# A two-block transformer kernel on one core: operand beginnings, the first weights, a joined recurrence step, and a new order of projections behind the attention

## The chip, the core and the metric

One core of a Trainium2 chip runs the whole program. Its engines are TensorE (PE, with PEld for the loading of weights), VectorE (DVE), ScalarE (ACT), GpSimd (POOL) and SyncE (SP), whose queue issues nearly all DMAs. The metric is the device time of one execution in microseconds (us). Before the change it is 1033.94, the median of three runs (1033.49 to 1034.37).

## What is computed

The input x has 512 positions and 1024 channels, batch 1, fp32. Two blocks follow each other:

```
def first_block(x, ...):
    h = rms_norm(x, g_mix)
    u, gb, gc, q, k, v = split(h @ w_in)
    y_conv = gb * short_conv(gc * u, conv_w)
    y_attn = dilated_mixture(q, k, v)
    x = x + concat(rms_norm(y_conv), rms_norm(y_attn)) @ w_out
    h = rms_norm(x, g_ffn)
    return x + (silu(h @ w_gate) * (h @ w_up)) @ w_down      # 2816 hidden channels

def second_block(x, c, ...):
    shift, scale, gate = split(silu(c) @ w_mod + b_mod)
    h = rms_norm(x) * (1 + scale) + shift
    xa, za, q, k, v, zb, qi, ki, wi, ga, gb = split(h @ w_in)
    ya = gelu(s5_mixer(xa, ...))                             # a complex state-space recurrence
    g = ya @ w_glu + b_glu
    ya = ((g[:, :512] * sigmoid(g[:, 512:])) * silu(za)) @ w_a_o
    yb = (dsa_mixer(q, k, v, qi, ki, wi) * silu(zb)) @ w_b_o # each query keeps its 128 best keys
    x = x + gate * ((sigmoid(ga) * ya + sigmoid(gb) * yb) @ w_out)
    return rms_norm(x, final_g)
```

## The kernel before

**Matrix products.** Nearly all of them run as three products in the type fp32r: a left and a right operand are each split into a high part and the rest, and `mm3` (L187 to L190) adds high x high, high x low and low x high into one PSUM accumulator. One such matmul has a 128x128 weight tile and a moving operand of 512 columns (256 in a few places). The moving operands have names by stage: xh/xl (first norm), fh/fl (feed-forward), th/tl (its hidden channels), hh/hl (second block), sh/sl (state-space output), ybh/ybl, yah/yal, mh/ml (the merged product). Each is a tile of 2048 bytes per partition, and where it begins in a partition follows from the order of the pools and the sizes of what lies in them. Worked out from these sizes, the operands begin at these bytes, modulo 512: the weights and the x, f, h parts at 416, th/tl at 160, sh/sl at 480, mh/ml at 352.

**Weights.** `units()` (L116) is a generator that loads weight blocks of 512 KB in a fixed order through SP (`load_w`, L113), and splits each on ACT (L92) and DVE (L93). `w()` hands out the next one and keeps three ahead; the tiles raw, wh and wl have three buffers each. The very first block is loaded in two halves by `first_w` (L96 to L107): the halves along the columns of the two row tiles that the block has are taken apart, each with its own cast and subtraction.

**Order of the work.** The order on TensorE is the order of the program. On the other engines and on SP a planner orders the instructions ahead of time by when it expects them to be ready, with a raised priority where the program says so. Waits on semaphores then decide when each instruction starts.

**First stage** (`mixer`, L304). Eight blocks x0 to x7 of the input, 256 KB each, come in through two buffers (L328, L329), and ACT and DVE make xh (L338) and xl (L339) of each. The keys' projection, 96 matmuls (L361 to L363), takes the blocks in that order, and with every two of them one weight block. Four small constants (L333 to L336) are issued behind x3.

**Feed-forward** (`ffn`, L554). 22 pairs of projections (j = 0 to 21). Beside them runs `ssm_tables`, a generator of small steps on POOL and DVE that builds the tables of the state-space part; `beside(gen, rate)` (L604) takes so many of its steps per row tile. At j = 0 the squares of the norm are gathered, at j = 2 the norm's factor is spread over the partitions (L226 to L231), and from there `finish` (L583 to L590) reads the accumulators.

**Second block** (`hybrid`, L978). The recurrence (L1121 to L1129) is 63 steps on POOL, each with four operations: a product of 64 columns (hm, L1125), a sum of 32 (hu, L1127), and two sums of 16 each (L1128, L1129) that cross the real and imaginary halves:

```
G.tensor_mul(m, H[:, c - 1, None].to_broadcast([P, 2, 2, 16]), ...)
G.tensor_add(u, m[:, 0], H[:, c])
G.tensor_add(H[:, c, 0], u[:, 0], m[:, 1, 1])
G.tensor_add(H[:, c, 1], u[:, 1], m[:, 1, 0])
```

Meanwhile TensorE runs the attention over four blocks of 128 queries with 8 heads each: scores sc (L249, L250), flips tp (L282), values (L295). Between these it takes steps of a filler, the generator `gates` (L1201 to L1218), at a rate set by `FILLE`; when the attention ends, `drain` takes what is left. `gates` has four projections for szb, four for sza, then the projections t0 to t4 (`tanhs(range(5))`), then four state-space outputs C0 to C3 (`chunk_out`), with t5 behind C0, t6 behind C1, t7 behind C2. One projection is 8 steps of three matmuls, one output chunk is 8 steps of two fp32 matmuls with 64 columns (L1172, L1173). C0 needs the whole recurrence (through the tile hs, L1160).

A chunk first loads two tables of 512 KB, cat (L1166) and tt (L1168), from DRAM through SP; both take the one tag "tab" with two buffers, and so each waits until the matmuls of the chunk before have read theirs. After its matmuls the result goes through ACT and DVE, is stored to DRAM in eight pieces (yad, L1184), read back (yl, L1186) and split into sh and sl (L1188 to L1191).

**Merge and end.** `pair(m)` (L1255) multiplies the attention's output with w_b_o, two columns of blocks at a time, and `glu` (L1263) multiplies sh/sl with w_glu. They run as pair 0, 1, 2, glu, pair 3. Then come the last gates and `pair` with ya, the product with w_out over mh/ml (L1293 to L1330), and the final norm in two halves of 256 positions (`norm`, L1343). Its factor goes through a chain of small DVE operations (L199 to L207), is spread by PE (L231), and multiplies the eight blocks: the first half on POOL with a copy Rs of the factor (L1363), the second on DVE out of PSUM (L1365).

Of the kernel before, what the change touches and what calls it, by code (L numbers as in the profile page):

```python
# [9 lines left out]
F = mybir.dt.float32  # L10
R = mybir.dt.float32r
# [23 lines left out]
class K:  # L35
# [8 lines left out]
    def pool(self, st, name, bufs=1, **kw):  # L44
        if "space" not in kw or kw["space"] == PSUM:
            kw.setdefault("reuse_waits", "tile")
        return st.enter_context(self.tc.tile_pool(name=name, bufs=bufs, **kw))


    def setup(self):  # L50
        nc, a, ctx = self.nc, self.a, self.ctx
        c = self.cpool = self.pool(ctx, "consts")
        self.wpool = self.pool(ctx, "weights")
        self.hpool = self.pool(ctx, "parts")
        self.ps = self.pool(ctx, "psum", space=PSUM)
        self.dram = ctx.enter_context(self.tc.tile_pool(name="scratch", bufs=1, space=DRAM))
        self.ones = c.tile([P, P], F, name="ones")
        self.G.memset(self.ones, 1.0)
        warm = c.tile([P, 1], F, name="warm")
        self.A.activation(warm, self.ones[:, 0:1], AF.Tanh)  # L60
        p = self.tp()
        for _ in range(WARM):
            self.T.matmul(p[:, :P], self.ones, self.ones, start=True, stop=True)
        self.cols = c.tile([P, NCOLS], F, name="cols")
        nc.scalar.dma_start(self.cols, a["cols"])
        self.ident = c.tile([P, P], F, name="ident")
        self.ident_r = c.tile([P, P], R, name="ident_r")
        self.cm = c.tile([P, P], F, name="cm")

    def col(self, name, j):  # L70
        o = COLS[name][0] + j
# [23 lines left out]

    def first_w(self):  # L96

        raw = self.wpool.tile([P, 2, S], F, name="raw", tag="raw", bufs=RAW)
        hi = self.wpool.tile([P, 2, S], R, name="wh", tag="wh", bufs=3)
        lo = self.wpool.tile([P, 2, S], R, name="wl", tag="wl", bufs=3)  # L100
        for k in range(2):
            src = self.a["wqkv"]
            ap = bass.AP(tensor=src.tensor, offset=src.offset + k * S, ap=[[2 * S, P], [1, S]])
            self.nc.sync.dma_start(raw[:, k], ap)
            self.A.copy(hi[:, k], raw[:, k])
            self.V.tensor_sub(lo[:, k], raw[:, k], hi[:, k].bitcast(F))
            yield hi, lo  # L107

    def load_w(self, name, off, kt, n):
        raw = self.wpool.tile([P, kt, n], F, name="raw", tag="raw", bufs=RAW)  # L110
# [5 lines left out]
    def units(self):  # L116

        def cols(name, c0, c1, kt, n):
            for c in range(c0, c1):
                yield self.split_w(self.load_w(name, c * P * kt * n, kt, n))  # L120
        yield from cols("wqkv", 1, 12, 2, S)
        yield from cols("wconv", 0, 12, 8, P)
        yield from cols("wout", 0, 8, 4, 256)
        yield from cols("wgu", 0, 44, 8, P)
        for n in range(8):
            for k0, kt in ((0, 8), (8, 8), (16, 6)):
                yield self.split_w(self.load_w("wdown", (n * 22 + k0) * P * P, kt, P))
        yield from cols("win2", 0, 5, 8, P)
        yield self.split_w(self.load_w("win2v", 0, 8, 72))
        yield from cols("win2", 5, 29, 8, P)  # L130
        yield from cols("wab", 4, 7, 4, 256)
        yield from cols("wglu", 0, 4, 4, 256)
        yield from cols("wab", 7, 8, 4, 256)
        for c in range(4):
            yield from cols("win2", 29 + 2 * c, 31 + 2 * c, 8, P)
            yield from cols("wab", c, c + 1, 4, 256)
        yield from cols("wout2", 0, 8, 8, P)
# [166 lines left out]
    def mixer(self):  # L304
# [16 lines left out]
        sq = sm.tile([P, S], F, name="sqA", tag="sq")  # L321
        first = self.first_w()
        for k in range(8):
            if k < 2:
                unit = next(first)
                if k:
                    self.ahead.append(unit)
            x = t1.tile([P, S], F, name="x", tag="x", bufs=2)  # L328
            nc.sync.dma_start(x, a["xT"][:, k * S:(k + 1) * S])  # L329
            if k in (2, 4):  # L330
                self.ahead.append(next(self.stream))
            if k == 4:
                nc.sync.dma_start(self.ident, a["ident"])  # L333
                nc.sync.dma_start(self.cm, a["cm"])
                nc.sync.dma_start(self.lc, a["lc"])
                nc.sync.dma_start(self.gqk, a["gqk"])  # L336
            g = self.col("g_mix", k)
            A.activation(xh[k], x, AF.Copy, scale=g)  # L338
            V.scalar_tensor_tensor(xl[k], x, g, xh[k].bitcast(F), op0=OP.mult, op1=OP.subtract)  # L339
            if k == 0:  # L340
                A.activation(sq, x, AF.Square)
            else:
                s2 = t1.tile([P, S], F, name="s2", bufs=2)
                A.activation(s2, x, AF.Square)
                G.tensor_add(sq, sq, s2)
        self.A.copy(self.ident_r, self.ident)
        self.mod_start()
        gqk = sm.tile([P, 64], F, name="gqk1")
        V.scalar_tensor_tensor(gqk, self.gqk[:, 0], 0.125, self.gqk[:, 1], op0=OP.mult, op1=OP.mult)
        rx = sm.tile([P, 4], F, name="rx")  # L350
# [203 lines left out]
    def ffn(self, x1):  # L554
# [49 lines left out]
        def beside(gen, rate):  # L604

            for _ in range(8):
                next(gen)
                pace[0] += rate
                if pace[0] >= 1:
                    pace[0] -= 1  # L610
                    next(table, None)
            return self.run(gen)
# [3 lines left out]
        for j in range(22):  # L616
            if j == 0:
                ws, first = [self.w() for _ in range(3)], [self.acc() for _ in range(3)]
                for js, ks in (((0, 1), range(4)), ((2,), range(4)), ((0, 1, 2), range(4, 8))):
                    for k in ks:  # L620
                        for q in js:
                            self.gemm(first[q], ws[q], xs, [k])
                with self.tc.high_priority(offset=LEAD):
                    r = self.rms(wk, [sq], D, "rf")
                continue
            if j == 1:
                first.append(beside(self.proj(xs), 0.25))
                continue
            if j == 2:
                pg = beside(self.proj(xs, self.acc2), 0.25)  # L630
                with self.tc.high_priority(offset=LEAD):
                    Rf = self.spread(wk, r, wk.tile([P, S], F, name="Rf"))
                pu = beside(self.proj(xs, self.acc2), 0.25)
                finish(0, *first[:2])
                finish(1, *first[2:])
                finish(2, pg, pu)
                continue
            ps = []
            for _ in range(2):
                t = self.proj(xs)  # L640
                ps.append(beside(t, 0.25 if j < 4 else 0.36))
            finish(j, *ps)
            if j > NT1:
                self.advance_mod()
# [333 lines left out]
    def hybrid(self, xs, second, close, out):  # L978
# [35 lines left out]
        ap = self.pool(aa, "attnE")  # L1014
        ss = ExitStack()
        ssp = self.pool(ss, "ssm", side="right")
        U = ssp.tile([P, 32, 64], F, name="U")
        H = ssp.tile([P, 64, 2, 16], F, name="H")
        s1 = ExitStack()
# [89 lines left out]
        def chunk_in():  # L1109
# [12 lines left out]
            for c in range(1, 64):  # L1122
                m = ssi.tile([P, 2, 2, 16], F, name="hm", bufs=2)
                u = ssi.tile([P, 2, 16], F, name="hu", bufs=2)
                G.tensor_mul(m, H[:, c - 1, None].to_broadcast([P, 2, 2, 16]),  # L1125
                             self.a8.rearrange("p (w r) g -> p w r g", w=2))
                G.tensor_add(u, m[:, 0], H[:, c])  # L1127
                G.tensor_add(H[:, c, 0], u[:, 0], m[:, 1, 1])  # L1128
                G.tensor_add(H[:, c, 1], u[:, 1], m[:, 1, 0])  # L1129


        def silu2(out, p):
# [68 lines left out]
        def gates():  # L1201
# [6 lines left out]
                for j in js:  # L1208
                    A.activation(thb[j], (yield from self.proj(xs)), AF.Tanh, scale=0.5)

            yield from tanhs(range(5))
            for _ in cin:
                pass
            s1.close()
            sso = self.pool(ss, "ssmout", side="right")
            for c in range(4):
                yield from chunk_out(sso, c)
                yield from tanhs(range(5 + c, min(6 + c, 8)))  # L1218

        sels = [sel, select(2), select(3)]  # L1220

# [60 lines left out]

        ya = []
        for m in range(4):
            if m == 3:
                glu()
            pair(yb, thb[2 * m:2 * m + 2], m, lambda n: thb[n])
        ss.close()
        m1 = thb

# [52 lines left out]
        def norm(e):  # L1343
# [15 lines left out]
                Rs = x3p.tile([P, S // 2], F, name="Rs")  # L1359
                A.copy(Rs, Rl)  # L1360
            for k in range(8):
                if e == 0:
                    G.tensor_mul(x3[k][:, t], x3[k][:, t], Rs)  # L1363
                else:
                    V.tensor_mul(x3[k][:, t], x3[k][:, t], Rl)  # L1365
                if k % 2:
                    nc.sync.dma_start(out.rearrange("(k p) t -> p k t", p=P)[:, k - 1:k + 1, t],
                                      x3t[:, k - 1:k + 1, t])

        for n in range(5, 8):  # L1370
            self.run(last(n, 0))
        self.run(last(5, 1))
        first, second = norm(0), norm(1)
        next(first)
        next(first)
# [108 lines left out]
```

## Time and profile before

| | before |
|---|---|
| median of three runs | 1033.94 us (1033.49 to 1034.37) |
| the profiled execution's own time | 1035.94 us |
| its span, first to last instruction | 1034.2 us |
| mean granted TensorE clock | 0.984 of 2.4 GHz |
| instructions | 13,924 |

The span is what the trace shows; 1.74 us of the profiled execution lie around it. The profiled execution is 2.0 us above the median of the runs. The busy time of a matmul in the trace reaches over the beginning of the next one, so the pace is read from starts, or from a stretch divided by the matmuls in it. A granted clock of 1.00 is 2.4 GHz, 0.50 is 1.2 GHz.

### The profile page before, as it was taken

How to read it: one execution, taken by the hardware profiler on the slowest of the kernel's cores; microseconds unless marked ns; L12 is line 12 of the kernel's file. 1: busy time of each engine (PE TensorE's matmuls, PEld its weight loads, DVE VectorE, ACT ScalarE, POOL GpSimd, SP SyncE). 2: the span in 40 equal slices, each digit the busy share in tenths (PEclk: the TensorE clock that was granted, in tenths of full speed). 3: DMA queues.
4: the chain of work that ended last, by engine and by line, in shares of the span. 5: the costliest groups of instructions: out<-in, count | busy, mean ns of one | idle time of the engine just before them, and what ended most of it. 6: DMA issues, size and time to landing. Idle time of an engine off the chain costs nothing.

```text
span 1034.2 us, 13924 instructions
## 1 busy us (share of the span) xinstructions
PE 998.9 (97%) x5074; PEld 824.7 (80%) x5074; DVE 687.2 (66%) x1315; ACT 424.7 (41%) x717; POOL 170.3 (16%) x393
## 2 busy tenths in 40 slices
PE   8999999999899999999999999999999699999995
PEld 6787777888787778888888898888887588788884
DVE  4876677886898757787743257799984355644434
ACT  6445556534234443233232235544444464433251
POOL 3020121005800000000010000001888200000022
PEclk9999999999999999999999999999999699999998
DMA  7233121124236547455543343373222154433212
GB/s 263 82 120 126 62 82 62 41 82 128 78 125 188 160 141 252 161 200 182 184 152 114 106 132 105 102 120 108 99 82 102 62 152 112 149 118 102 82 42 82
DMA packets 55572, 125.12 MB, mean 121 GB/s; under 512 B 17424, under 2 KB 24080, under 8 KB 55376
## 3 DMA queue, kind: packets, MB, share of 16 engines
q1 hardware_dynamic: 55360, 124.19, 37.7%
q8 instruction: 40, 0.66, 0.3%
q14 instruction: 28, 0.23, 0.1%
q10 hardware_dynamic: 144, 0.05, 0.0%
HBM read 110.45 MB, written 12.58 MB: 119 GB/s over the span
## 4 chain that ended last, share of the span: by engine, by line
PE 71%; POOL 10%; DVE 10%; DMA 3%; issue 3%; ACT 3%; SPq 1%; DVEq 0%; POOLq 0%; ACTq 0%
PE acc L188 19%; PE acc L189 19%; PE acc L190 19%; POOL hm L1125 3%; DVE wl L93 2%; POOL H L1128 2%; POOL hu L1127 2%; PE acc L363 2%; PE acc L361 2%; PE acc L362 1%; DMA x<-in_xT 1%; POOL H L1129 1%; PE acc L295 1%; PE tp L282 1%; POOL stt L719 1%
## 5 line engine op out<-in xcount | busy, mean ns | idle before, releaser
L92 ACT CAST wh<-raw 128x1024 fp32r<-128x1024 f32 x157 | 162.5, 1036 | 286.2 <-PE acc L189 238.4
L93 DVE TENSOR_TENSOR wl<-raw,wh 128x1024 fp32r<-128x1024 f32 x157 | 194.2, 1238 | 89.2 <-ACT wh L92 87.7
L188 PE MATMUL acc<-fh,wh 128*128 128x512 f32 x336 | 133.1, 396 | 1.4 <-DVE gs L585 1.4
L189 PE MATMUL acc<-fl,wh 128*128 128x512 f32 x336 | 130.9, 390 | 0.0
L190 PE MATMUL acc<-fh,wl 128*128 128x512 f32 x336 | 130.8, 389 | 0.0
L188 PE MATMUL acc<-hh,wh 128*128 128x512 f32 (+1 forms) x280 | 114.3, 408 | 0.0
L190 PE MATMUL acc<-hh,wl 128*128 128x512 f32 (+1 forms) x280 | 110.1, 393 | 0.0
L189 PE MATMUL acc<-hl,wh 128*128 128x512 f32 (+1 forms) x280 | 109.9, 392 | 0.0
L188 PEld LDWEIGHTS acc<-fh,wh 128*128 128x128 f32 x336 | 63.1, 188 | 16.3 <-issue 1.9
L190 PEld LDWEIGHTS acc<-fh,wl 128*128 128x128 f32 x336 | 63.1, 188 | 13.5
L189 PEld LDWEIGHTS acc<-fl,wh 128*128 128x128 f32 x336 | 63.1, 188 | 12.7 <-issue 0.2
L188 PE MATMUL acc<-th,wh 128*128 128x512 f32 (+1 forms) x198 | 72.6, 367 | 0.0
L189 PE MATMUL acc<-tl,wh 128*128 128x512 f32 (+1 forms) x198 | 72.3, 365 | 0.0
L190 PE MATMUL acc<-th,wl 128*128 128x512 f32 (+1 forms) x198 | 72.3, 365 | 0.0
L190 PEld LDWEIGHTS acc<-hh,wl 128*128 128x128 f32 (+1 forms) x280 | 52.5, 187 | 12.3
L257 ACT ACTIVATE e<-z,mn 128x128 f32<-128x128 f32 (+3 forms) x64 | 36.0, 562 | 63.9 <-DVE mn L253 63.4
L188 PEld LDWEIGHTS acc<-hh,wh 128*128 128x128 f32 (+1 forms) x280 | 52.7, 188 | 10.7 <-issue 1.4
L189 PEld LDWEIGHTS acc<-hl,wh 128*128 128x128 f32 (+1 forms) x280 | 52.8, 189 | 8.7
L1125 POOL TENSOR_TENSOR hm<-H,a 128x64 f32<-128x64 f32 x63 | 25.8, 410 | 125.7 <-DVE H L243 120.9
L666 POOL TENSOR_TENSOR sqD<-sqD,s 128x512 f32<-128x512 f32 x6 | 8.4, 1394 | 208.6 <-ACT s L653 208.6
L189 PEld LDWEIGHTS acc<-tl,wh 128*128 128x128 f32 x198 | 37.3, 189 | 6.1
L188 PEld LDWEIGHTS acc<-th,wh 128*128 128x128 f32 x198 | 37.3, 189 | 6.0
(402 smaller groups left out, 2153.6 us busy)
## 6 DMA issues: line engine op xcount, KB each, us to landing
raw<-in_wgu SPq DMA_DIRECT2D x44, 512.0 KB, 3.6
raw<-in_win SPq DMA_DIRECT2D x37, 512.0 KB, 3.6
mraw<-in_wmod SPq DMA_DIRECT2D x24, 512.0 KB, 4.6
raw<-in_wout SPq DMA_DIRECT2D x16, 512.0 KB, 3.5
raw<-in_wdown SPq DMA_DIRECT2D x16, 512.0 KB, 3.4
raw<-in_wconv SPq DMA_DIRECT2D x12, 512.0 KB, 3.5
raw<-in_wqkv SPq DMA_DIRECT2D x11, 512.0 KB, 4.1
x<-in_xT SPq DMA_DIRECT2D x16, 256.0 KB, 5.2
```

The lines of the kernel that those rows point to most:

```text
L92: self.A.copy(hi, raw)
L93: self.V.tensor_sub(lo, raw, hi.bitcast(F))
L188: self.T.matmul(out, lh, rh, start=start, stop=False)
L189: self.T.matmul(out, lh, rl, start=False, stop=False)
L190: self.T.matmul(out, ll, rh, start=False, stop=stop)
L257: self.A.activation(e[:, :n], z[:, :n], AF.Exp, bias=mn, scale=-1.0, accum_out=den)
L282: self.T.transpose(pp[:, j * P:(j + 1) * P], e[:, j * P:(j + 1) * P], self.ident)
L361: T.matmul(ps[i], xh[k][:, t], wh[:, kk], start=k == 0, stop=False)
L363: T.matmul(ps[i], xl[k][:, t], wh[:, kk], start=False, stop=k == 7)
L1125: G.tensor_mul(m, H[:, c - 1, None].to_broadcast([P, 2, 2, 16]), self.a8.rearrange("p (w r) g -> p w r g", w=2))
L1127: G.tensor_add(u, m[:, 0], H[:, c])
L1128: G.tensor_add(H[:, c, 0], u[:, 0], m[:, 1, 1])
```

## The change

- A helper `pad` puts a dummy tile on POOL into four pools (constants 96 bytes, smallA 448, ssm 480, x3E 352), so that the pools and tiles behind it begin at multiples of 512 bytes.
- `first_w` loads the first two weight blocks in four pieces of 256 KB, one per row tile and half; the input blocks get three buffers; the third weight block is issued at k = 4, and the four small constants at k = 7. The order of the wab and wglu blocks follows the new order of the merge.
- The feed-forward's projection j = 1 runs without table steps, and j = 3 takes 0.5 steps per row tile where it took 0.25.
- The two 16-column sums of the recurrence become one of 32 columns with a reversed operand.
- `gates` takes t0 to t6 ahead of C0; t7 follows C0, and C1, C2, C3 follow without a projection between them.
- The four attention pairs run ahead of `glu`.
- The final norm's first half is multiplied on DVE (with Rs) instead of POOL.

```diff
+    def pad(self, pool, size):
+        self.G.memset(pool.tile([P, size // 4], F, name="pad"), 0.0)
...
     def first_w(self):
-        raw = self.wpool.tile([P, 2, S], F, name="raw", tag="raw", bufs=RAW)
-        hi = self.wpool.tile([P, 2, S], R, name="wh", tag="wh", bufs=3)
-        lo = self.wpool.tile([P, 2, S], R, name="wl", tag="wl", bufs=3)
-        for k in range(2):
-            src = self.a["wqkv"]
-            ap = bass.AP(tensor=src.tensor, offset=src.offset + k * S, ap=[[2 * S, P], [1, S]])
-            self.nc.sync.dma_start(raw[:, k], ap)
-            self.A.copy(hi[:, k], raw[:, k])
-            self.V.tensor_sub(lo[:, k], raw[:, k], hi[:, k].bitcast(F))
-            yield hi, lo
+        src = self.a["wqkv"]
+        for c in range(2):
+            raw = self.wpool.tile([P, 2, S], F, name="raw", tag="raw", bufs=RAW)
+            hi = self.wpool.tile([P, 2, S], R, name="wh", tag="wh", bufs=3)
+            lo = self.wpool.tile([P, 2, S], R, name="wl", tag="wl", bufs=3)
+            for k in range(2):
+                ap = bass.AP(tensor=src.tensor, offset=src.offset + (c * P * 2 + k) * S, ap=[[2 * S, P], [1, S]])
+                self.nc.sync.dma_start(raw[:, k], ap)
+                self.A.copy(hi[:, k], raw[:, k])
+                self.V.tensor_sub(lo[:, k], raw[:, k], hi[:, k].bitcast(F))
+                yield hi, lo
...
-        yield from cols("wab", 4, 7, 4, 256)
+        yield from cols("wab", 4, 8, 4, 256)
         yield from cols("wglu", 0, 4, 4, 256)
-        yield from cols("wab", 7, 8, 4, 256)
...
-            if k < 2:
+            if k < 4:
                 unit = next(first)
-                if k:
+                if k % 2:
                     self.ahead.append(unit)
-            x = t1.tile([P, S], F, name="x", tag="x", bufs=2)
+            x = t1.tile([P, S], F, name="x", tag="x", bufs=3)
...
-            if k in (2, 4):
+            if k == 4:
                 self.ahead.append(next(self.stream))
-            if k == 4:
+            if k == 7:
                 nc.sync.dma_start(self.ident, a["ident"])
...
             if j == 1:
-                first.append(beside(self.proj(xs), 0.25))
+                first.append(self.run(self.proj(xs)))
...
-                ps.append(beside(t, 0.25 if j < 4 else 0.36))
+                ps.append(beside(t, 0.5 if j < 4 else 0.36))
...
-                G.tensor_add(H[:, c, 0], u[:, 0], m[:, 1, 1])
-                G.tensor_add(H[:, c, 1], u[:, 1], m[:, 1, 0])
+                G.tensor_add(H[:, c], u, m[:, 1, ::-1])
...
-            yield from tanhs(range(5))
+            yield from tanhs(range(7))
...
                 yield from chunk_out(sso, c)
-                yield from tanhs(range(5 + c, min(6 + c, 8)))
+                yield from tanhs(range(7 + c, 8))
...
         for m in range(4):
-            if m == 3:
-                glu()
             pair(yb, thb[2 * m:2 * m + 2], m, lambda n: thb[n])
+        glu()
...
             for k in range(8):
-                if e == 0:
-                    G.tensor_mul(x3[k][:, t], x3[k][:, t], Rs)
-                else:
-                    V.tensor_mul(x3[k][:, t], x3[k][:, t], Rl)
+                V.tensor_mul(x3[k][:, t], x3[k][:, t], Rl if e else Rs)
```

## Rows read from the trace of the kernel before

**Rows 1.** The page's first part: busy time and share of the span of each engine.

```profile
PE 998.9 (97%) x5074; PEld 824.7 (80%) x5074; DVE 687.2 (66%) x1315; ACT 424.7 (41%) x717; POOL 170.3 (16%) x393
```

**Rows 2.** Waits of TensorE: line waiting, what ended it, us in total, times, longest.

```profile
PE acc L1172 <- POOL hs L1160: 10.3, 1, 10.3
PE tp L231 <- DVE rey L205: 5.4, 2, 5.0
...
PE acc L361 <- ACT xh L338: 2.2, 3, 1.1
PE tp L282 <- ACT qT L241: 1.9, 1, 1.9
PE acc L188 <- DVE gs L585: 1.4, 1, 1.4
PE tp L231 <- DVE sc_p L777: 1.3, 1, 1.3
...
PE acc L189 <- DVE sl L1191: 0.6, 1, 0.6
```

**Rows 3.** Windows: length, PE, PEld, DVE, ACT, POOL busy (count), PE clock, DMA share, GB/s.

```profile
5.33:31.13 25.80, 24.15 (x97) 17.42 (x97) 14.63 (x18) 16.65 (x26) 9.93 (x7) 1.00 0.72 247
116.80:124.00 7.20, 5.28 (x19) 4.01 (x18) 5.84 (x13) 4.16 (x9) 2.19 (x1) 0.76 0.22 73
282.87:304.63 21.76, 21.76 (x97) 18.02 (x96) 21.76 (x30) 8.14 (x12) 0.92 (x2) 1.00 0.35 121
802.90:823.40 20.50, 13.43 (x53) 12.26 (x54) 7.42 (x20) 8.87 (x18) 5.88 (x25) 0.50 0.21 74
809.95:819.59 9.64, 9.62 (x42) 9.24 (x43) 3.85 (x10) 3.70 (x9) 0.00 (x0) 0.50 0.15 56
830.33:835.52 5.19, 5.19 (x45) 5.02 (x44) 3.46 (x10) 4.26 (x9) 0.00 (x0) 1.00 0.49 145
857.44:860.93 3.49, 3.49 (x34) 3.49 (x32) 3.48 (x8) 3.24 (x6) 0.00 (x0) 1.00 0.50 65
982.88:999.68 16.80, 16.80 (x74) 13.54 (x73) 6.67 (x7) 8.63 (x16) 4.66 (x3) 1.00 0.21 63
```

**Rows 4.** Timeline of SP in the first stage: start, length, the third input block's issue.

```profile
6.14 0.33 SPq L329 DMA_DIRECT2D x<-in_xT  x1
```

**Rows 5.** POOL by line: the first of the recurrence's two sums.

```profile
L1128 POOL TENSOR_TENSOR H<-hu,hm 128x16 f32<-128x16 f32 x63 | 18.1, 287 | 4.9
```

**Rows 6.** Timeline of SP behind chunk C1, and the landing of all tt tables.

```profile
835.88 0.43 SPq L1168 DMA_DIRECT2D tt<-tabs  x1
842.11 3.83 SPq L1184 DMA_DIRECT2D yad<-ys  x8
847.63 0.34 SPq L1186 DMA_DIRECT2D yl<-yad  x1
...
DMA to landing us min/median/max: 4.5/5.0/5.7
```

**Rows 7.** Timeline of DVE in the feed-forward: a table step with its wait.

```profile
268.98 0.26 DVE L840 TENSOR_SCALAR snr<-pr 128x48 f32<-128x48 f32 x1 [4.41 <-POOL pr L811]
```

**Rows 8.** Timeline of the final norm: one DVE step of each half, then both multiplications.

```profile
1014.03 0.17 DVE L200 TENSOR_SCALAR rey<-rev 128x2 int32<-128x2 int32 x1
...
1023.41 0.65 DVE L200 TENSOR_SCALAR rey<-rev 128x2 int32<-128x2 int32 x1
...
1019.89 5.49 POOL L1363 TENSOR_TENSOR x<-x,Rs 128x256 f32<-128x256 f32 x8 [16.79 <-ACT Rs L1360]
...
1028.10 2.74 DVE L1365 TENSOR_TENSOR x<-x,tp 128x256 f32<-128x256 f32 x8 [1.38 <-PE tp L231]
```

**Rows 9.** Groups of PE matmuls by form, of L188 alone (L189, L190 alike).

```profile
L188 PE MATMUL acc<-fh,wh 128*128 128x512 f32 x336 | 133.1, 396 | 1.4 <-DVE gs L585 1.4
...
L188 PE MATMUL acc<-hh,wh 128*128 128x512 f32 x272 | 111.1, 409 | 0.0
...
L188 PE MATMUL acc<-mh,wh 128*128 128x512 f32 x40 | 15.8, 395 | 0.0
```

More of the change, by code (lines that the diff above doesn't have):

```diff
@@ L68, in setup @@
         self.cm = c.tile([P, P], F, name="cm")
+        self.pad(c, 96)
     def col(self, name, j):
@@ L120, in cols @@
                 yield self.split_w(self.load_w(name, c * P * kt * n, kt, n))
-        yield from cols("wqkv", 1, 12, 2, S)
+        yield from cols("wqkv", 2, 12, 2, S)
         yield from cols("wconv", 0, 12, 8, P)
@@ L347, in mixer @@
         self.mod_start()
+        self.pad(sm, 448)
         gqk = sm.tile([P, 64], F, name="gqk1")
@@ L1016, in hybrid @@
         ssp = self.pool(ss, "ssm", side="right")
+        self.pad(ssp, 480)
         U = ssp.tile([P, 32, 64], F, name="U")
@@ L1372, in hybrid @@
         self.run(last(5, 1))
+        self.pad(x3p, 352)
         first, second = norm(0), norm(1)
```

## The prediction

> **What bounds the kernel now.** I read the busy time first: TensorE is busy for 97% of the span, every other engine far less [rows 1], so a change pays only where TensorE stands still, where its clock is down, or where a matmul takes longer than it must. The table of TensorE's waits says where it stands still: one wait of 10.3 us of the first chunk matmul (L1172) for hs, 5.0 us at the end for the norm's factor, 2.2 us in three waits for the input, and 1.3 and 1.4 us at the start of the feed-forward [rows 2]. The windows say where the clock is down: behind the 10.3 us wait the granted clock is 0.50, the lower level of 1.2 GHz, for 20.5 us [rows 3], and C0's piece takes 9.64 us where C1's, which holds as many matmuls of the same kinds, takes 5.19 at 1.00 [rows 3]. A much shorter wait, 1.9 us of L282 [rows 2], is also followed by a fall: 0.76 over the 7.20 us around it [rows 3]. So a wait of TensorE has two prices, its own length and the slow work behind it. The pace comes last: 96 matmuls of 512 columns in 21.76 us are 226.7 ns each in a steady stretch, and 72 in 16.80 us over mh/ml 233.3 [rows 3] (a record or two over that number overlap the edges).
>
> **Part by part, against the profiled execution's own 1035.94 us.**
>
> *A, the start.* The keys' 96 matmuls take 25.80 us, where 96 x 0.2267 = 21.76 would do [rows 3]: 4.0 us are lost, 2.2 of them in three waits for xh [rows 2]. The third block's load is issued only at 6.14 us [rows 4], because it needs a buffer that x0 holds. With three buffers it goes out right behind the sixth piece, and the pieces by row tile put 256 KB less in front of it; the constants, now behind the last block, are out of the way too. Against that, SP issues two DMAs more, and ACT and DVE each make two smaller pieces of what was one. Bounds: 0 and -4.0. I take **-2.0**, nearly the row of waits.
>
> *B, table steps in the feed-forward.* The waits of 1.3 and 1.4 us [rows 2] come while DVE sits in front of table steps that wait for POOL, one of them 4.41 us with `finish` queued behind it [rows 7]. Without steps beside j = 1 these are later; but the planner may put them in front of the norm or of `finish` all the same, and the doubled rate at j = 3 brings them closer together. Bounds: both waits gone, -2.7, or one more like the longer, +1.4. I take **-0.6**, the middle.
>
> *C, the order behind the attention.* Counting the filler's steps, TensorE now runs t5 and t6, with attention between, ahead of C0: together some 16 us, as t5 and t6 hold 48 matmuls of 512 columns, 48 x 0.2267 = 10.9 us, and the attention the rest. hs was 10.3 us late, so that wait goes, whatever the joined sum costs: it replaces two, of which the first takes 18.1 us over 63 steps [rows 5] and the second about as much, and even were it as long as both, 16 us cover it. This part is **-10.3**. With it goes the slow clock: 9.64 - 5.19 = 4.45 us at C0, and in t5 the 3.8 us from 819.6 to 823.4 that ran at half, so 1.9 us: **-6.35**.
>
> What is late next? C2 and C3 now follow directly on C1 and C2, and cat and tt share two buffers. C1's piece ends at 835.52 [rows 3]; at once SP issues cat, at 835.88 tt, and tt lands 5.0 us later (4.5 to 5.7) [rows 6]. So far t6 and t7 covered that; now nothing stands between, so TensorE waits some 5.2 us twice: **+10.4** (0.36 + 4.5 to 0.36 + 5.7 each: 9.7 to 12.2). The splitting into sh/sl and the copies into hs fit beside it. Each wait also has the second price. The 1.9 us wait cost 7.20 x 0.24 = 1.7 us of clock, the 10.3 us one 6.35 [rows 3]; at 5.2 us a straight line between these gives 3.5, an estimate, twice **+7.0**, which C2, C3 (3.49 us of matmuls [rows 3]) and the first pair would pay. Bounds: 3.4 and 12.7. A fourth pair, 24 matmuls or 5.4 us, now stands between C3 and `glu`, so the wait for sl goes: **-0.6** [rows 2]. C's sum: -10.3 - 6.35 + 10.4 + 7.0 - 0.6 = **+0.15**, bounds -4 and +8.
>
> *D, the end.* In the second half's norm the first four DVE steps take some 0.65 us where the same take 0.17 in the first half, while POOL multiplies (5.49 us) [rows 8]: 4 x 0.48 = 1.9 us on the path of the 5.0 us wait [rows 2]. On DVE the eight products take 2.74 / 8 = 0.34 us each [rows 8]. Some fit ahead of the second half's chain; of the others one or two may stand in it. **-1.2**, bounds -1.9 and -0.5. The four stores of that half leave earlier and hold nobody.
>
> *E, beginnings.* If mh/ml step at 226.7 in place of 233.3 ns, the 3 x 40 full matmuls [rows 9] give 120 x 6.6 = **-0.8**; bounds 0 and -1.0 with a little for sh/sl. Below that see the third rival: no operand in this trace begins at a multiple of 64 bytes, so the pace at 0 is not shown. The four memsets lie on POOL, which is idle for 84% of the span [rows 1]; alone they cost nothing.
>
> *The rest* is the recurrence itself, 9 us earlier on POOL, hidden behind t5 and t6; if these did not cover it, hs would be the wait again.
>
> Sum: -2.0 - 0.6 + 0.15 - 1.2 - 0.8 = **-4.45**, so 1031.5 for the profiled execution. That one stands 2.0 above the median of the runs, so the forecast is **1029.5**. A measurement of this kernel can tell some 0.2%, 2.07 us, from no change: the bounds are 1031.9 and 1036.0.
>
> **The rivals.**
>
> *The clock holds, or the tables are hidden.* If no slow work follows the two table waits, C is -6.85 and the time 1029.5 - 7.0 = 1022.5. Against it: the waits of 1.9 and of 10.3 us were each followed by a fall [rows 2, 3]. If the tables also came in time, it would be 1012.1; but the two buffers exclude a load before the chunk's last matmul, and tt was issued 0.36 us behind it [rows 3, 6].
>
> *SP's queue (slower).* SP issues in a fixed order. If the planner expects C1's result stores before C2's end of reading, cat and tt of the next chunk stand behind the eight yad stores and yl, which were issued 6.6 to 12.1 us behind a chunk's end [rows 6]. Then tt lands at 12.1 + 0.7 + 5.0 = 17.8 us instead of 5.4: +12.4 once, and 1029.5 + 12.4 = 1041.9, slower. It decides from a delay of 6.5 us on, as then the sum passes +2.07. For it: between the chunks lies now less time than the stores take to be ready, so at C3 they are close. Against it: the trace has tt 6.2 us ahead of yad [rows 6].
>
> *The pace (faster).* The pace depends on where a moving operand begins: 226.7 ns at 416 and 233.3 at 352 modulo 512 [rows 3], with the weights at the same place. All of them lie at 32 modulo 64, and the change brings nearly all to 0. If that takes away what is above the 512 columns at 2.4 GHz, 213.3 ns, each matmul gains up to 13.4 ns; fh and hh alone are 3 x (336 + 272) = 1824 [rows 9], so up to -24 us from them and 1005 us; with the other groups lower still. For it: the difference of 6.6 ns exists. Against it: 416 and 160 differ in their place and step alike at 226.7, so the excess may be the weights' or a fixed one. The Trainium skill, "TensorE: Matmul & The Clock Gate", section "Back-to-back issue gap", gives N/2.4 + 2.5 ns, which is 215.8 for 512 columns, and with no condition on where an operand begins; the measured 226.7 stands above it. By that page the sum would be 1824 x 10.9 = -20 us lower from these two groups, 1010. The same section's sustained 131 ns for 512 columns is contradicted by every row here.
>
> *The change does less than it says.* If the planner puts the table steps and the products where they were, B and D are 0, and the forecast becomes 1031.3; this lies within the likeliest case.
>
> **How the numbers follow.** The likeliest, table waits in the stall's place with a slow clock behind them: 0.52, its own range 1024 to 1038 (C from -4 to +8 with the other terms at their values, 1025 to 1037, and a little for these). By its centre I put 0.30 of it below 1031.9, 0.14 between the bounds and 0.08 above. Clock holds or tables hidden: 0.15. Pace: 0.14. SP's queue: 0.15, of which 0.03 is a short delay that ends between the bounds; 0.04 stay for what I don't see, half and half between no difference and slower. Faster 0.59, same 0.19, slower 0.22. The range of 1012 to 1040 leaves out the full pace gain (most of 0.14) and the longer half of the queue's delays (about 0.06).
>
> **What would show it.** Of A: L361's waits gone and the keys' stretch near 23.8 us. Of C: no wait for hs at C0, but two of about 5 us at L1172 or L1173 in front of C2 and C3, ended by tabs, and a granted clock of 0.50 behind them; with the first rival the clock stays at 1.00, with SP's queue cat is issued behind yl. Of D: L199 to L202 at 0.17 us in both halves. Of B: less than 2.7 us in the two feed-forward waits. Of E: mh's stretch of 72 matmuls at 16.3 us; for the pace rival fh's stretch of 96 below 21 us, and that alone would make the forecast wrong by ten and more us.

## The result, and the profile after

The changed kernel takes 1052.84 us (median of four runs, 1050.60 to 1053.51), beside 1033.92 before (four runs here): a ratio of 1.018, 95% interval 1.0164 to 1.0196. It is slower by 18.9 us, where 4.4 us less were forecast, and outside the range. The profiled execution took 1052.63 us, its span is 1050.8. The two profiled executions lie 16.7 us apart, less than the medians, as the one before stands 2.0 above its median.

TensorE's waits after (line waiting, what ended it, us in total, times, longest), to be read beside [rows 2]. Lines are the changed kernel's: L287 is L282 before (a flip, that is a transposition of e on PE), L236 is L231, L903 is L897, L1178 is L1172.

```profile
PE tp L287 <- DVE e L265: 8.2, 2, 8.0
PE acc L1178 <- DMA cat<-tabs: 5.9, 1, 5.9
PE tp L903 <- ACT bts L904: 4.2, 1, 4.2
PE tp L236 <- DVE rey L210: 3.6, 2, 3.2
PE acc L1178 <- ACT ybh L1259: 3.4, 1, 3.4
...
PE tp L1356 <- ACT s L1345: 2.1, 1, 2.1
...
PE acc L193 <- DVE gs L591: 1.5, 1, 1.5
PE tp L236 <- DVE sc_p L783: 1.3, 1, 1.3
```

The wait for hs is gone, and one nearly as long, 8.0 us, stands at a flip of the attention, which waits for e. Two waits for the tables are new (the 3.4 us at L1178 is also C3's, though it is put down to ybh: cat was issued at 866.58 and PE went on at 870.17; in experiment 1 both are put down to cat, 9.3 us). One of 4.2 us in the feed-forward is new too.

Windows after (columns as in [rows 3]):

```profile
5.31:29.05 23.74, 22.87 (x96) 17.82 (x97) 20.41 (x18) 16.42 (x26) 11.32 (x7) 1.00 0.77 266
329.30:336.10 6.80, 5.12 (x19) 3.53 (x20) 3.30 (x4) 3.45 (x8) 0.36 (x1) 0.50 0.32 128
428.49:450.25 21.76, 21.76 (x98) 18.02 (x96) 17.88 (x26) 6.80 (x10) 0.00 (x0) 1.00 0.54 193
800.30:810.50 10.20, 5.78 (x16) 4.86 (x17) 4.88 (x14) 5.89 (x13) 2.42 (x9) 0.50 0.09 34
851.50:865.20 13.70, 9.02 (x54) 8.74 (x56) 2.94 (x7) 4.02 (x6) 0.00 (x0) 0.50 0.37 112
868.60:882.30 13.70, 11.67 (x43) 10.55 (x44) 5.01 (x9) 5.38 (x9) 0.09 (x1) 0.50 0.27 91
992.63:1008.95 16.32, 16.32 (x74) 13.52 (x73) 6.44 (x7) 7.55 (x13) 2.94 (x2) 1.00 0.29 94
```

Each of the four long waits has a stretch at 0.50 with it. In the three of the second block PE is busy for 5.78 + 9.02 + 11.67 = 26.5 us, which at the full clock would be about 12.4 less (a step of 512 columns takes 427 ns there, by the starts from 878.71 to 881.27, beside 226.7). Before it was 13.43 us in one stretch, 6.3 lost.

Where the time went is read from the same matmul in both traces, start against start. At the end of the keys the changed kernel is 2.1 us ahead, at 300 us 2.2 ahead, at 400 us 4.2 behind, at 790 us 4.3 behind, at the beginning of the last gates (906 before, 923 after) 17.5 behind, at the last product's 256-column halves 16.7 to 17.2, at the end of the span 16.6. So two places cost: +6.5 between 300 and 400, +13.2 between 790 and 906.

The wait for the flip, which ends inside the window from 800.30, looks like this (POOL, ACT, DVE and PE of the timeline; start, length, line; in brackets the idle time before and what ended it):

```profile
801.67 0.25 POOL L1135 TENSOR_TENSOR H<-hu,hm 128x32 f32<-128x32 f32 x1
...
801.95 1.24 ACT L246 COPY hs<-H 64x252 f32<-64x252 f32 x2 [13.61 <-POOL H L1135]
803.22 0.61 ACT L262 ACTIVATE e<-z,mn 128x384 f32<-128x384 f32 x1
...
801.95 0.82 DVE L248 COPY hs<-H 64x252 f32<-64x252 f32 x2 [11.50 <-POOL H L1135]
803.96 0.16 DVE L264 RECIPROCAL rd<-den 128x1 f32<-128x1 f32 x1 [1.19 <-ACT e L262]
804.15 0.42 DVE L265 TENSOR_SCALAR e<-e,rd 128x384 f32<-128x384 f32 x1
...
804.72 0.88 PE L287 MATMUL tp<-ident,e 128*128 128x128 f32 x3 [7.97 <-DVE e L265]
```

DVE stands for 11.5 us, not for lack of work, but because the next instruction of its queue is a copy into hs, which needs the recurrence up to its last step but one. ACT stands for 13.6 us in the same way. The softmax's e goes through both engines, its exponent on ACT (L262) and then its division on DVE (L264, L265), and each part is behind that engine's copies. This is not new. Before the change DVE's lines were these:

```profile
808.30 0.84 DVE L243 COPY hs<-H 64x252 f32<-64x252 f32 x2 [13.07 <-POOL H L1129]
809.17 0.17 DVE L259 RECIPROCAL rd<-den 128x1 f32<-128x1 f32 x1
809.37 0.42 DVE L260 TENSOR_SCALAR e<-e,rd 128x384 f32<-128x384 f32 x1
```

PE's wait was put down to hs then, since C0 came first on PE; the flip that follows C0's first step was held by the same copy: e was done at 809.79, and C0 began at 809.97. With other work in C0's place PE would have stood at the flip nearly as long.

### The profile page after: what moved, and what is told of

The parts are those of the page before. It is cut to its first block, busy times and chain, and to the rows that moved or that the text cites. A ratio compares the mean times of both kernels' runs of the same rounds, so it can differ in the third digit from the quotient of the medians.

```text
span 1050.8 us, 13873 instructions
## 1 busy us (share of the span) xinstructions
PE 1005.9 (96%) x5074; PEld 833.2 (79%) x5074; DVE 693.6 (66%) x1324; ACT 423.8 (40%) x718; POOL 155.8 (15%) x326
## 4 chain that ended last, share of the span: by engine, by line
PE 74%; DVE 10%; POOL 9%; issue 3%; DMA 2%; ACT 1%; SPq 0%; DVEq 0%; POOLq 0%; ACTq 0%
PE acc L193 19%; PE acc L194 19%; PE acc L195 19%; POOL hm L1132 2%; DVE wl L98 2%; POOL hu L1134 2%; POOL H L1135 2%; PE acc L369 2%; PE acc L367 2%; PE acc L368 2%; PE acc L300 2%; PE tp L287 1%; DMA tt<-tabs 1%; PE acc L1179 1%; PE acc L1178 1%
## 5 line engine op out<-in xcount | busy, mean ns | idle before, releaser
L193 PEld LDWEIGHTS acc<-fh,wh 128*128 128x128 f32 x336 | 63.5, 189 | 16.6 <-issue 2.1
L262 ACT ACTIVATE e<-z,mn 128x128 f32<-128x128 f32 (+3 forms) x64 | 36.0, 562 | 58.7 <-DVE mn L258 58.3
L195 PEld LDWEIGHTS acc<-th,wl 128*128 128x128 f32 x198 | 37.3, 188 | 6.0
```

Source lines behind the costliest of these rows:

```text
L193: self.T.matmul(out, lh, rh, start=start, stop=False)
L195: self.T.matmul(out, ll, rh, start=False, stop=stop)
L262: self.A.activation(e[:, :n], z[:, :n], AF.Exp, bias=mn, scale=-1.0, accum_out=den)
```

## The experiments

All are edits of the changed kernel if nothing else is said. Medians stand beside that of the kernel before on the same chip, which was 1034.4 to 1036.4; the ratios are to it. "Less" and "more" without another name are against the changed kernel's 1052.84, which was not run again beside them. Runs of one kernel spread by up to 6.6 us (before: 1033.08 to 1039.66), so a difference of 2 us says little, and the single runs of experiments 2 and 4 count by their traces.

**1. The old table rates.**

```diff
-                first.append(self.run(self.proj(xs)))
+                first.append(beside(self.proj(xs), 0.25))
...
-                ps.append(beside(t, 0.5 if j < 4 else 0.36))
+                ps.append(beside(t, 0.25 if j < 4 else 0.36))
```

> The changed kernel with the feed-forward's table rates of before (0.25 at j = 1 and j = 3), nothing else undone. Theory (the faster rate brings the second table's transposes ahead of the landing of the first table's tt store, and PE then waits for the copy bts behind it): the wait of 4.2 us at L903 goes, and with it the half clock of 6.8 us behind it, so about 6.5 us less than the changed kernel, near 1046. Rival (the loss in the feed-forward comes from the pads or from the shifted start, not from the rate): the wait stays and the time is that of the changed kernel, 1052.8.

1045.6 us (1041.6 to 1047.5), 7.2 less; no wait at L903 above 1 us, and no half clock there. The theory holds as to the place.

**2. Two buffers for bts and tt**, at the new rates. These are two tiles of the table building; they share the tag io, which has one buffer.

```diff
-            bts = p.tile([P, 8, P], F, name="bts", tag="io")
+            bts = p.tile([P, 8, P], F, name="bts", tag="io", bufs=2)
...
-            tt = p.tile([P, 8, P], F, name="tt", tag="io")
+            tt = p.tile([P, 8, P], F, name="tt", tag="io", bufs=2)
```

> The changed kernel with two buffers for the tiles bts and tt of the table building (tag io), rates as changed. Theory (bts of the second table has to wait for the store of the first table's tt, which shares its one buffer): the wait of 4.2 us at L903 goes at the new rates too, about 6.5 us less than the changed kernel. Rival (the wait is for DMA in general, the weights loaded in the same microseconds): the wait stays at 3 us or more.

1045.9 us in one run, 6.9 less, and L903 is gone from the waits; behind the tables it is 2.4 us ahead of before, start against start, where the changed kernel is 4.2 behind. So the cause is the one buffer: the second table's copy bts waits for the first table's tt to be stored. In the changed kernel that store was issued by SP at 322.30, with three weight blocks around it, and ACT stood until 330.34:

```profile
330.34 0.58 ACT L904 COPY bts<-tp 128x512 f32<-128x512 f32 x1 [7.11 <-DMA raw<-in_wgu]
```

The releaser named is a weight load. The view of the store's own line (L925) names the copy as what waited for it, and a longest landing of 7.8 us, which from 322.30 ends at 330.1:

```profile
  ACT bts L904: 5.0, 2
...
DMA to landing us min/median/max: 4.3/6.1/7.8
```

Before, the same copy waited for the store too, but only for 0.34 us:

```profile
331.44 0.59 ACT L898 COPY bts<-tp 128x512 f32<-128x512 f32 x1 [0.34 <-DMA tabs<-tt]
```

It was done at 332.03, half a us ahead of PE's next transposes for it (L897, 332.52). At the new rate these were due at 326.75.

**3. The first chunk's copies into hs on POOL.**

```diff
-                    self.copy(hs[64 * ri:64 * ri + 64, e:8:2, 1:],
+                    (G.tensor_copy if c == 0 else self.copy)(
+                        hs[64 * ri:64 * ri + 64, e:8:2, 1:],
```

> The changed kernel with the four copies into hs of the first chunk on POOL instead of ACT and DVE. Theory (the planner put these copies ahead of the attention's work in the fixed queues of ACT and DVE, and both engines stand there until the recurrence ends, so PE waits for e): the 8.0 us wait of PE for e at L265 goes and the half clock behind it too, about 2.9 us of work; 9 to 11 us less than the changed kernel, near 1042 to 1044. Rival (the recurrence itself holds the attention, or the wait for e has another cause): the wait stays, or comes back at C0 as a wait for hs of the same length.

1040.64 us (1038.7 to 1044.1), 12.2 less, a little more than expected. The wait for e is gone (0.3 us) and none for hs has come, though the four copies take 3.64 us on POOL. The blocked queues are shown.

**4. Two sums again in the recurrence.**

```diff
-                G.tensor_add(H[:, c], u, m[:, 1, ::-1])
+                G.tensor_add(H[:, c, 0], u[:, 0], m[:, 1, 1])
+                G.tensor_add(H[:, c, 1], u[:, 1], m[:, 1, 0])
```

> The changed kernel with the recurrence's last step as two sums of 16 columns again, as before the change. Theory of the blocked queues: the recurrence ends some 8 to 9 us later, and the wait for e grows from 8.0 to about 16 to 17 us, with the half clock behind it not shorter: 9 to 12 us more than the changed kernel. Rival (the copies are placed by when the planner expects the recurrence to end, so with four operations it puts them later): the wait for e goes or shrinks, and the time falls by up to 10 us.

1048.52 us in one run, 4.3 less, against my theory and with the rival: the wait for e is 4.9 us instead of 8.0, although the recurrence ends later. In the trace DVE's copy into hs starts at 809.32. Counted in the timelines, 22 of the second block's 32 divisions of e on DVE and 23 of its 32 exponents on ACT stand ahead of the copies here, exactly as in the kernel before; in the changed kernel it is 19 and 19. So the joined sum put the copies three and four steps of the attention further ahead. This fits a planner that places the copies by when it expects the recurrence to end; no run sets its order by hand, so the planner's reason stays an inference. (Start against start, 2.5 us of the gain lie between 790 and 906 and 1.6 between 300 and 400, where the feed-forward's wait is 3.4 instead of 4.2.)

**5. The joined sum alone**, on the kernel before.

```diff
-                G.tensor_add(H[:, c, 0], u[:, 0], m[:, 1, 1])
-                G.tensor_add(H[:, c, 1], u[:, 1], m[:, 1, 0])
+                G.tensor_add(H[:, c], u, m[:, 1, ::-1])
```

> The kernel before with the joined sum alone, nothing else changed. Theory of the blocked queues: the recurrence ends 9 us earlier, the planner puts the copies into hs a little earlier in the queues of ACT and DVE, and as C0 follows at once on PE, the wait falls from 10.3 to 2 to 4 us whichever instruction of PE carries it; with less half clock behind it 8 to 12 us less than before, 1022 to 1026. Rival (the copies move ahead by more than the recurrence gains): the wait is 7 us or more, at L265 instead of L1172, and the time is within 4 us of before.

1030.07 us (1028.7 to 1033.8), ratio 0.9946. The rival was right on the mechanism, and the time lies between: the wait is 7.6 us, and it is at L282 for e, no longer at L1172 for hs. ACT's copies start at 797.05, 11 us earlier than before, with 19 exponents and 19 divisions ahead of the copies in place of 23 and 22, and the wait falls by 2.7 us alone.

**6. The joined sum and the copies on POOL**, on the kernel before.

The edit is that of experiment 5 with that of experiment 3.

> The kernel before with two edits, the joined sum and the first chunk's copies into hs on POOL. Theory of the blocked queues: ACT and DVE go on with the attention while the recurrence ends, so the wait for e of 7.6 us that the joined sum alone showed goes; C0 then waits for hs itself, as the recurrence ends near 798.3 and the four copies take 3.6 us there, 2 to 4 us at L1172, and less clock is lost than before. 5 to 9 us less than the joined sum alone, 1021 to 1026. Rival (the copies' place doesn't matter, the recurrence's end sets when PE goes on): 1029 to 1031 as with the joined sum alone.

1028.07 us (1026.2 to 1030.5), 2 less than the joined sum alone, and their ranges overlap (start against start it is 1.9 less between 790 and 906); the expectation of 5 to 9 was too much. The waits came as foreseen, 2.5 us for hs at L1172 and 0.3 for e, but a stretch of 10.2 us at half clock followed all the same.

**7. Cover between the chunks**: pair 0 between C2 and C3, the projections one place later than before.

```diff
-            yield from tanhs(range(7))
+            yield from tanhs(range(6))
...
-            for c in range(4):
-                yield from chunk_out(sso, c)
-                yield from tanhs(range(7 + c, 8))
+            for c in range(3):
+                yield from chunk_out(sso[0], c)
+                yield from tanhs(range(6 + c, min(7 + c, 8)))
...
+            if m == 0:
+                self.run(chunk_out(sso[0], 3))
```

> The changed kernel with another order behind the attention: t0 to t5 ahead of C0, t6 behind C0, t7 behind C1, C2 behind it, then pair 0, then C3, then pairs 1 to 3 and glu, so that work stands between any two chunks. Theory (the two waits for tables are there because nothing lies between the chunks): the waits of 5.9 and 3.4 us at L1178 go, and with them two stretches of half clock of 13.7 us each, some 10 us of work; a wait for the last sl of 1 to 2 us may come. 18 to 21 us less than the changed kernel, near 1033, with the wait for e still there. Rival (the tables' landing is late for another cause, a full SP queue or slow DMA): waits for cat or tt stay at C2 or C3 and less than 8 us is won.

1038.76 us (1036.7 to 1040.5), 14.1 less, 4 short of the expectation. Both table waits are gone, but pair 0 came so early that PE waited 2.8 us for ybh and 1.5 for ybl, with 6.8 us of half clock. The tables' landing itself was no hindrance.

**8. The chunks in the order of before.**

```diff
-            yield from tanhs(range(7))
+            yield from tanhs(range(5))
...
-                yield from tanhs(range(7 + c, 8))
+                yield from tanhs(range(5 + c, min(6 + c, 8)))
```

> The changed kernel with the order of before among projections and chunks (t0 to t4, C0, t5, C1, t6, C2, t7, C3); the rest of the change stays, pairs ahead of glu too. Theory: the two table waits and their half clock go, the wait for hs or e at C0 is 2 to 8 us, the feed-forward's wait of 4.2 us stays; 16 to 24 us less than the changed kernel, 1029 to 1037. Rival (the order is not what costs; the loss is the clock, which falls in any order): less than 8 us is won.

1031.05 us (1028.4 to 1033.0), 21.8 less: the order of the chunks alone costs more than the change lost in all. What stays is 7.3 us for e and 4.4 at L903. That wait for e is 7.3 to 8.0 us, with 19 exponents and 19 divisions ahead of the copies, in all seven profiles that have the joined sum and the copies on ACT and DVE (the changed kernel, experiments 1, 2, 5, 7, 8 and 11), whatever the order of projections and chunks.

**9. Combined**: edits 1 and 3, and an order with cover for every chunk.

```diff
-            yield from tanhs(range(7))
+            yield from tanhs(range(6))
...
+            yield from chunk_out(sso, 0)
+            yield from tanhs([6])
+            yield from chunk_out(sso, 1)
+            t7 = tanhs([7])
+            for _ in range(4):
+                next(t7)
+                yield
+            yield from chunk_out(sso, 2)
+            yield from t7
+            yield from chunk_out(sso, 3)
```

> The changed kernel with the old table rates, with the first chunk's copies into hs on POOL, and with t0 to t5 ahead of C0, t6 behind C0, four steps of t7 behind C1 and four behind C2, so that every chunk's tables have cover. Theory (the three losses are separate: the rate, the blocked queues, the bare tables): the wait at L903, the wait for e at L265 and the waits for cat of 3 to 6 us are all gone or at most 1 us each, and no half clock stretch stands between 700 and 900 us; that is 7.2 + 12.2 + some 20 less than the changed kernel, near 1014, range 1010 to 1020. Rival (one wait takes the place of another, as PE is fed by the same chain of tables, hs and yb): one wait of more than 3 us and its half clock stay, and the time is 1022 to 1032.

1025.38 us (1023.2 to 1027.0), ratio 0.9893 (0.9869 to 0.9917); the rival was right, one wait at the edge of its 3 us. Between C2 and C3 PE waited 3.0 us for cat and 0.8 for tt, with 10.2 us at half clock. SP's timeline shows what the prediction's rival of SP's queue describes, on a small scale:

```profile
834.49 3.79 SPq L1191 DMA_DIRECT2D yad<-ys  x8
838.40 1.73 SPq L1173 DMA_DIRECT2D cat<-tabs  x1
```

C2's last matmuls were done at 835.76, 2.6 us before; cat stood behind C1's eight stores.

**10. Combined, the cover laid out otherwise**: t6 is halved around C1, t7 stands whole between C2 and C3.

```diff
+            yield from chunk_out(sso, 0)
+            t6 = tanhs([6])
+            for _ in range(4):
+                next(t6)
+                yield
+            yield from chunk_out(sso, 1)
+            yield from t6
+            yield from chunk_out(sso, 2)
+            yield from tanhs([7])
+            yield from chunk_out(sso, 3)
```

> The combined version once more with the cover laid out otherwise: t0 to t5 ahead of C0, four steps of t6 behind C0, four behind C1, the whole of t7 (5.4 us of matmuls) behind C2; the rest as in the first combined version. Theory (what is left there is the wait of 3.0 and 0.8 us for C3's tables with 10.2 us of half clock, as t7's four steps of 2.7 us and the stores ahead of cat in SP's queue left it short): the wait falls to 2 us or less and the half clock goes, 4 to 9 us less than the first combined version, 1017 to 1022. Rival (SP's queue: cat and tt of C3 stand behind the stores of C1 and the reading back, whatever lies on PE): the wait of 3 us or more stays, 1023 to 1027.

1017.04 us (1016.9 to 1018.3), ratio 0.9818 (0.9801 to 0.9835): faster than both kernels. The first part of its page and its window over the whole stretch:

```profile
PE 991.3 (98%) x5074; PEld 821.6 (81%) x5074; DVE 693.5 (68%) x1322; ACT 424.2 (42%) x716; POOL 161.5 (16%) x330
...
790.00:890.00 100.00, 99.31 (x608) 84.42 (x607) 59.19 (x115) 52.43 (x89) 12.88 (x36) 1.00 0.38 122
```

PE is busy for 99.31 of 100 us at the full clock, with 0.7 us for one tt left.

**11. The same with the copies back on ACT and DVE.**

The edit undoes that of experiment 3 in the version of experiment 10.

> The second combined version with the first chunk's copies into hs back on ACT and DVE; order, rates and all else as there. Theory of the blocked queues: the order alone doesn't help, as the copies stand ahead of the attention's work in both queues whatever PE has in hand; the wait for e at L265 of 7 to 8 us comes back with a stretch of half clock of 7 to 10 us, 9 to 13 us more than the second combined version, 1026 to 1030. Rival (with a projection and a half more cover ahead of C0 the copies would have been harmless, and the gain of the combined version came from the order): within 3 us of 1017.

1027.88 us (1026.6 to 1030.6), 10.8 more than experiment 10. The wait for e is back, 7.3 us with 10.2 us of half clock, and start against start 10.7 us are lost between 790 and 906. So the order does not cover what stands in another engine's queue.

## Why the prediction was wrong, by its own steps

In the profiled executions -4.45 us were forecast and +16.7 came. B accounts for 7.1 us of the difference, C for 13.0, D and E for 1.1. A, D and E have no run of their own and are read from the changed kernel's trace.

*A, the start:* right in size. The keys' stretch takes 23.74 us, 23.8 was said, and -2.1 came for -2.0. The sign was half there: the three waits for the input did not go, they fell from 2.2 to 1.3 us, and so "nearly the row of waits" is not what made the size.

*B, the table steps:* wrong, +6.5 for -0.6 and outside its bounds. I weighed the two waits that the trace had, and both are still there (1.5 and 1.3). What failed is the bound "one more like the longer, +1.4": the higher rate brings not only table steps closer together, but PE's transposes of the second table ahead of a store's landing. That cost 4.2 us of wait and, by the steps, some 2.4 us of half clock, for which B had no term. The row for it existed before, the copy at 331.44, which already waited 0.34 us for the store.

*C, the order:* here lies most of the error. The step "so that wait goes, whatever the joined sum costs" failed: -10.3 was booked and -2.3 came (8.0 in place of 10.3). The working asked only what PE has to do ahead of C0, and not where the copies into hs stand in the queues of ACT and DVE. The attention, with which t5 and t6 are interleaved on PE, needed those two engines (experiments 3 and 11). And the joined sum, which the step set aside, moved the copies further ahead (experiments 4 and 5); with two sums the new order leaves 4.9 us. The trace of before showed the queue: 13.07 us of idle DVE in front of a copy with e behind it.

The table waits were right in their cause and their sum, 5.9 and 3.4 us and 0.9 for tt, 10.2 for +10.4; that the sum fits so well is partly luck, as it is 6.3 and 3.9 for 5.2 twice. The clock was mis-sized: I took +7.0 for the two waits by a line between a short and a long one; the two stretches hold 9.02 + 11.67 = 20.7 us of busy PE, some 9.7 us lost, about midway between that and the upper bound of 12.7. And the -6.35 for the old stretch was booked in full, though the wait for e brought a stretch of its own, 2.7 lost. C came to +13.2 for +0.15: 8.0 from the stall, 5.5 from the clock (12.4 - 6.3 = 6.1 in place of 0.65), and some 0.4 less in the rest.

*D, the end:* right in the mechanism, mis-sized. The wait for the norm's factor fell from 5.0 to 3.2 us, but the wait in front of it rose from 1.0 to 2.1: four of the first half's products stand on DVE ahead of the last block's sum, where one or two were allowed for. The first steps (L204 to L207) take 0.16 to 0.17 us in both halves, as said. About -0.6 for -1.2.

*E, beginnings:* right in size for the full matmuls, 16.32 us for 72 as said, 0.7 us in all, but the 256-column halves of mh/ml, which I left out, went the other way and gave some 0.4 us of it back.

*The rivals.* The pace rival fell: 96 matmuls over fh take 21.76 us, exactly as before [rows 3]. The formula of the Trainium skill, "TensorE: Matmul & The Clock Gate", section "Back-to-back issue gap", N/2.4 + 2.5 ns, gives 215.8 ns for 512 columns. That isn't reached here with any beginning that was run. That the clock holds fell too: 0.50 behind both table waits. SP's queue did not happen in the changed kernel (cat at 849.64, yad at 855.85), but did in experiment 9.

## What to carry to other kernels

Ahead of counting work as cover for a wait, look at the queue of every engine which that work needs: an instruction that waits for the late result, placed ahead, turns the cover into a second wait, and the profile names only the one that PE meets first. An idle stretch of DVE or ACT with a releaser from a slow chain is the row to read; putting the waiting copies on the engine that makes the result took the block away. A shorter chain can be worth less than it gains, where a planner moves its users forward with it (in experiment 5 the recurrence ended 11.5 us earlier and the kernel 5.2), and an order that packs like with like has to be checked for the loads that the old one hid.

## What the runs showed that I had not expected

With the pads the pace changed only in some forms. Over mh, whose beginning moved from 352 to 0 modulo 512 by the sizes, a matmul of 512 columns went from 233.3 to 226.7 ns, but one of 256 columns from 118 or 113.5 to 120.0 by the starts; over fh, from 416 to 0, nothing changed (226.7). The three profiles without pads (before, experiments 5 and 6) have the old pace over mh, all those with pads the new one. No run has the pads alone, so that the beginning is the cause is argued.

A wait of 3.4 us was followed by as long a stretch at half clock, 13.7 us, as one of 5.9 us, and in experiment 6 one of 2.5 us by 10.2 us. So the clock's share of a wait is not in proportion to its length, and a short wait can cost more behind it than in itself. Nor is it the same for the same wait. The 1.9 us for qT in the first block (L282 before, L287 after) is in all thirteen profiles, and it was followed by 3.4 us of half clock in eight of them and by none in five; the 7.3 us for e by 6.8 us in two and by 10.2 in three. A price of the clock read from one profile, as in the prediction, is therefore one draw of several.
